# Low parts of 35 weight tiles made by an accumulating DMA in place of a subtraction, in a one-core encoder block

## The chip, the cores and the metric

The kernel runs on one core of a Trainium2 chip. The metric is the device time of one execution in microseconds (us), taken as the median of several runs. The core's engines are TensorE (PE, the matmuls; PEld is its loading of weights), VectorE (DVE), ScalarE (ACT), GpSimd (POOL) and SyncE (SP, which only issues transfers). Each works through its own queue in order; they meet at semaphores. Transfers between device memory and on-chip memory (DMA) run on 16 shared DMA engines and are issued here mostly by SP, a few by GpSimd and ScalarE.

## The reference

One layer of an encoder for 512 tokens of 1024 channels, all in 32-bit floats:

```python
h = _rmsnorm(x, norm_mix[i])
proj = h @ w_in[i]                       # 1024 -> 768 + 256 + 32 + 3 * 512
q = (_rmsnorm(c_q, q_norm[i]) @ w_uq[i])  # latent attention, 8 heads of 96
kv = (_rmsnorm(c_kv, kv_norm[i]) @ w_ukv[i])
y_attn = _block_attention(q, k, v)
y_hyena = x0 * _bidir_long_conv(x1 * vh, h_fwd, h_bwd, hyena_bias[i])
x = x + concat(norm(y_attn), norm(y_hyena)) @ w_out[i]
x = x + (silu(g) * u) @ w_down[i]        # g, u: convolved halves of norm(x) @ w_up
x = x + sigmoid(x @ w_ple_gate[i]) * _rmsnorm(p[i] @ w_ple[i], ple_norm[i])
```

So there are an input projection, attention with a normed latent query and key, a long convolution whose filter comes from a small network (three sine layers), an output projection for both halves, a gated MLP, and an embedding gate.

## The kernel before

**Precision.** TensorE works on `float32r` operands, which hold fewer bits than `float32`. Every matrix operand is therefore cut in two: a high part `hi`, rounded to `float32r`, and a low part `lo = raw - hi`. A product is three matmuls: `hi hi`, `hi lo`, `lo hi` (`prod3`). A tile of weights has 128 partitions and up to 1024 columns; 8 blocks of 128 columns, three matmuls each, are 24 matmuls of 512 tokens.

**The stream of weights.** `stream` lists all weight tiles in the order of use, each with a number of columns `cut`. Tiles 0 to 20 are the input projection (tiles 0 and 1 are loaded in halves by other code at the start), 21 is the keys' projection, 22 to 27 are the queries' (768 columns), 28 is the values', 29 to 36 are the output projection (first the four tiles of the convolution's half, then the four of attention's), 37 to 80 are the MLP's projection up, and then come the projection down, the embedding and the gate. `wload` handles one tile: SP loads it into a raw buffer (L138), ScalarE rounds it into `hi` (L141, named wh in the profile), and the low part (wl) is subtracted, columns up to `cut` on VectorE (L143), the others on GpSimd (L145). For tiles 2 to 36 the list `CUTS` divides the columns between the two engines; from tile 37 on VectorE does all.

**Buffers and lead.** There are three raw buffers and two each for `hi` and `lo`, so the rounding of a tile has to wait until TensorE is done with the tile before the last one. `next_w` hands out a tile and asks for the next one by `ahead(i + 2)`. The filter's output weights (L401) and the transposed embedding take a raw buffer too.

**The order of work.** TensorE's queue is written out by hand: matmuls of the projections, with tasks between them (filter network, transforms, statistics) that come in after a given time of TensorE's, then the attention over eight heads with pieces of the output projection between, then the MLP. The orders on VectorE, ScalarE, GpSimd and SP come from a scheduler that goes by priority; `wload` runs at a priority raised by `WPRI` from the fifth tile on. GpSimd also issues the transfers of the transform's matrices (dft, L499 and L503), `sel` and `selT`, and does products and sums for the convolution, the rotation and the softmax.

**Names that recur.** L175 is the line of all products (`mms`), L131 and L134 are subtractions in `split`, which makes high and low parts of activations, L365 and L375 are a sine layer's matmul and its sine, L412 is the low half of its last output, L403 and L404 sum the filter's output weights, L437 scales the filter in time (the waits of L551 name it), L551 is the transposes for the transform, L596 to L608 are sums after it, L645 and L646 are squares of the latent query, L665 copies the sums of squares that L230 turns, L219 sums squares over channels, L486 to L492 are squares of x.

Of the kernel before, what the change touches and what calls it, by code (L numbers as in the profile page):

```python
# [12 lines left out]
F32 = mybir.dt.float32  # L13
F32R = mybir.dt.float32r
AF = mybir.ActivationFunctionType
ALU = mybir.AluOpType
# [3 lines left out]
P = 128  # L20
# [41 lines left out]
GN = (4, 6, 7, 9)  # L62
CPRI = 50
EPS = 1e-6
NH = 8
# [23 lines left out]
def tile_encoder_block(  # L89
# [6 lines left out]
    V, S, G, PE, SP = nc.vector, nc.scalar, nc.gpsimd, nc.tensor, nc.sync  # L96
# [8 lines left out]
    const = ctx.enter_context(tc.tile_pool(name="const", bufs=1))  # L105
    apool = ctx.enter_context(tc.tile_pool(name="apool", bufs=16))
    wpool = ctx.enter_context(tc.tile_pool(name="wpool", bufs=2))
# [20 lines left out]
    def split(hi, lo, src, g=None):  # L128
        if g is None:
            S.activation(hi, src, AF.Copy)  # L130
            V.tensor_tensor(lo, src, f32(hi), op=ALU.subtract)  # L131
        else:
            S.activation(hi, src, AF.Copy, scale=g)
            V.scalar_tensor_tensor(lo, src, g, f32(hi), op0=ALU.mult, op1=ALU.subtract)  # L134

    def wload(src, n, cut):
        raw = wpool.tile([P, 1024], F32, tag="wr", name="wr", bufs=3)
        SP.dma_start(raw[:, :n], src)  # L138
        hi = wpool.tile([P, 1024], F32R, tag="wh", name="wh")
        lo = wpool.tile([P, 1024], F32R, tag="wl", name="wl")  # L140
        S.activation(hi[:, :n], raw[:, :n], AF.Copy)  # L141
        if cut:
            V.tensor_tensor(lo[:, :cut], raw[:, :cut], f32(hi[:, :cut]), op=ALU.subtract)  # L143
        if cut < n:
            G.tensor_tensor(lo[:, cut:n], raw[:, cut:n], f32(hi[:, cut:n]), op=ALU.subtract)  # L145
        return hi, lo

    stream = [(w_in[m], 1024, CUTS[m]) for m in range(21)]
# [3 lines left out]
    for m in range(8):  # L152
        stream += [(w_down[m][:, o * P : (o + nk) * P], nk * P, nk * P) for o, nk in ((0, 8), (8, 8), (16, 6))]
        if m == 6:
            stream += [(w_ple[0], 1024, 1024), (w_ple[1], 1024, 1024)]
    stream += [(w_gate[m], 1024, 1024) for m in range(8)]
    ready = []
    taken = [0]

    def ahead(i):  # L160
        while len(ready) < min(i, len(stream)):
            with tc.high_priority(offset=WPRI if len(ready) > 3 else 0):
                ready.append(wload(*stream[len(ready)]))

    def next_w():
        i = taken[0]
        taken[0] += 1
        if i:
            ahead(i + 2)
        return ready[i]  # L170
# [29 lines left out]

    # out = v ** -0.5 for v = src / n + EPS
    def rsqrt(out, v, w, src, n, key):
# [19 lines left out]

    # statistics with the tokens on partitions: column 8 t + h for token tile t and head h
    def col(name="col"):
# [21 lines left out]

# [1 line left out]
    p2 = ExitStack()  # L248
# [8 lines left out]
    def single(name, shape=(P, T), dt=F32):  # L257
        return ft.tile(list(shape), dt, tag=name, name=name)

    def first_tile():  # L260
        return [
            wpool.tile([P, 1024], dt, tag=g, name=g, bufs=n)
            for g, dt, n in (("wr", F32, 3), ("wh", F32R, 2), ("wl", F32R, 2))
        ]
# [11 lines left out]
    xraw, halves = [], {}  # L276
    for k in range(8):
        t = xpool.tile([P, T], F32, tag="x", name="x")
# [12 lines left out]
    for k in range(8):  # L291
        h, l = atile(), atile()
# [11 lines left out]
    accx, accy = single("accx"), single("accy")  # L304
# [20 lines left out]
    sel = const.tile([P, 56], F32R, tag="sel", name="sel")  # L325
    selT = const.tile([40, 6, P], F32R, tag="selT", name="selT")

    # work beside the projections: each task continues after the tensor engine's given time
    tasks, clock, serial = [], [0.0], itertools.count()
# [23 lines left out]

    # rotary key part (replicated in the four 32-row groups)
    def rotate(dst, src):
# [5 lines left out]

    # long filter: network, last layer, decay, transform
    def sin_layer(hin, kk, col, bcol):
# [19 lines left out]

    # sums and differences of the even samples' halves, at k = 2p and k = 255 - 2p
    def fold_even(cs, a, b, d0, d1):
# [9 lines left out]
    def filter_task():  # L395
        h = sin_layer(zc[0:33, :], 33, 0, "b1")
        yield D_SIN
        h = sin_layer(h[0:64, :], 64, 1, "b2")
        fw_hl = []
        fwo = wpool.tile([P, 1024], F32, tag="wr", name="wr", bufs=3)  # L400
        SP.dma_start(fwo, fw_out)  # L401
        for op in (ALU.add, ALU.subtract):
            t = tmp()  # L403
# [5 lines left out]
        h = sin_layer(h[0:64, :], 64, 2, "b3")  # L409
# [15 lines left out]
        for i, cs in ((0, "c"), (1, "s")):  # L425
            eo = []
            for jt in range(4):
                ps = filt(i, jt)
                t = tmp()
# [9 lines left out]
                if jt < 2:  # L439
                    h, l = gtile(), gtile()  # L440
# [5 lines left out]
            s, d = tmp(), tmp()  # L446
# [5 lines left out]
            for x, t in ((2, s), (3, d)):  # L452
                h, l = gtile(), gtile()
# [30 lines left out]
    for k in range(8):  # L484
        sq = (accx, accy)[k] if k < 2 else tmp()
        S.activation(sq, xraw[k], AF.Square)  # L486
        if k >= 2:
            if k % 2 == 0:
                last = G.tensor_tensor(accx, accx, sq, op=ALU.add)
# [41 lines left out]

    # hyena projections with their short convolution
    def conv(c, z, w, b, m):
# [12 lines left out]
    def transform_task():  # L546
# [33 lines left out]
        while len(H) < 8:  # L580
            yield 1.0
        # product with the filter's transform
        for j in range(2):
# [14 lines left out]
            yield D_MUL  # L598
        # sums for the inverse's halves
        gce, gco = [U["c", j] for j in range(2)], [U["c2", j] for j in range(2)]  # L600
# [32 lines left out]

    # latent q
    zq = []
# [11 lines left out]

    # queries
    act_table("natural_log_exp_and_others")

    def square(src):
        with pri("sq"):
            sq = single("sq")
            S.activation(sq, src, AF.Square)
            h, l = tmp(F32R), tmp(F32R)
            split(h, l, sq)
        return h, l
# [20 lines left out]

    # keys
    wk = next_w()  # L680
# [95 lines left out]

    # values, token-major, high and low parts beside each other
    wv = next_w()
# [113 lines left out]

# [1 line left out]
    p1 = ExitStack()  # L894
# [144 lines left out]

# [1 line left out]
    fp = ctx.enter_context(tc.tile_pool(name="fp", bufs=1, reuse_waits="tile"))  # L1041
# [28 lines left out]

    # projection down, with the per-layer embedding's projection before its last tile
    ev = []

    def embedding():
        ptr = wpool.tile([P, 1024], F32, tag="wr", name="wr", bufs=3)
        SP.dma_start(ptr, pT)
        ph, pl = (fp.tile([P, 1024], F32R, tag=g, name=g) for g in ("ph", "pl"))
        split(ph, pl, ptr)
        pp = [(ph[:, i * T : (i + 1) * T], pl[:, i * T : (i + 1) * T]) for i in range(2)]
        for m in range(8):  # L1080
            if m % 4 == 0:
                w = next_w()
            ps = ax_ps()
            mms(ps, prod3(wtiles(w, 2, (m % 4) * 256), pp))
            em = tf()
            S.activation(em, ps, AF.Copy)
            if m == 0:
                S.activation(acc7, ps, AF.Square)
            else:
                sq = tt4()  # L1090
                S.activation(sq, ps, AF.Square)  # L1091
                G.tensor_tensor(acc7, acc7, sq, op=ALU.add)  # L1092
            ev.append(em)
# [18 lines left out]
    for m in range(8):  # L1112
# [9 lines left out]
        t = tt4()  # L1122
# [174 lines left out]
```

## Time and profile before

| | |
|---|---|
| Median of three runs | 774.98 us (774.70 to 776.65) |
| Span of the profiled execution, first to last instruction | 774.3 us |
| TensorE busy | 730.1 us (94%) |
| VectorE busy | 531.5 us (69%) |
| ScalarE busy | 356.4 us (46%) |
| GpSimd busy | 250.5 us (32%) |
| DMA, bytes moved | 74.84 MB, 97 GB/s on average |

The page of the profile gives the span of the profiled execution, and no other time of it; the median of the runs lies 0.7 us above that span. A row of a group of instructions reads: line, engine, operation, tiles written and read, shapes, count, busy time and mean of one, and the idle time of the engine just before them with what ended it. A row of the waits reads: engine, tile and line that waited, what it waited for, us in total, times, longest. A row of the stretches has from and to, the length, and for PE, PEld, DVE, ACT and POOL the busy us with the count of instructions; then the granted clock of TensorE as a share of full speed, the busy share of the DMA engines, and GB/s. A row of the order in time has the start, the length, engine, line and tiles, and in brackets the idle time before it. A row of the DMA issues has the count, the size of one and the median us from issue to landing.

### The profile page before, as it was taken

The page shows a single profiled execution, that of the slowest core. Times are in us where ns is not written, and L with a number is a line of the kernel's source. Part 1 is how long each engine was busy: PE and PEld are TensorE (multiplying, and loading weights), DVE is VectorE, ACT ScalarE, POOL GpSimd, SP SyncE. Part 2 cuts the span into 40 slices and gives each one's busy share as a digit, 9 for nine tenths or more (in the row PEclk, how much of TensorE's full clock was granted, in tenths as well). Part 3 has the DMA queues.
Part 4 walks back from the last instruction along what each step waited for, and adds up shares of the span by engine and source line. Part 5 has one row for each costly group of instructions (what it writes and reads, how often), then busy time and mean ns, then how long its engine had stood idle before and what let it go on. Part 6 is the DMA issues. An engine that isn't in the chain of part 4 may idle for free.

```text
span 774.3 us, 8973 instructions
## 1 busy us (share of the span) xinstructions
PE 730.1 (94%) x3254; PEld 584.7 (76%) x3254; DVE 531.5 (69%) x729; ACT 356.4 (46%) x543; POOL 250.5 (32%) x201
## 2 busy tenths in 40 slices
PE   6987989988798989999999999999999999999997
PEld 4765778765467777777888888888888888888886
DVE  6499998899879989786866656666565333233383
ACT  6443343334757977354554443434444122226341
POOL 4356542567355665232232122212222000005000
PEclk9999999989899999999999999999999999999999
DMA  8622332211244210022323232332323333333331
GB/s 280 212 81 83 112 106 83 66 50 41 82 129 115 84 50 28 34 98 89 101 88 109 86 105 87 105 106 85 108 82 103 95 86 108 91 124 102 108 109 55
DMA packets 25504, 74.84 MB, mean 97 GB/s; under 512 B 3402, under 2 KB 3978, under 8 KB 25459
## 3 DMA queue, kind: packets, MB, share of 16 engines
q1 hardware_dynamic: 24418, 71.62, 29.1%
q0 software_dynamic: 784, 2.25, 0.9%
q8 instruction: 25, 0.41, 0.2%
q10 hardware_dynamic: 256, 0.39, 0.2%
q14 instruction: 21, 0.16, 0.1%
HBM read 69.01 MB, written 2.10 MB: 92 GB/s over the span
## 4 chain that ended last, share of the span: by engine, by line
PE 53%; DVE 0%; ACT 0%; DVEq 0%; issue 0%
PE mm L175 36%; PE ax L175 17%; PE ax L219 0%; DVE t L1125 0%; ACT t L1124 0%; DVEq L1292 0%; DVE t L1126 0%
## 5 line engine op out<-in xcount | busy, mean ns | idle before, releaser
L175 PE MATMUL mm<-a,wh 128*128 128x512 f32 (+1 forms) x928 | 291.3, 395 | 8.7 <-ACT wh L272 5.4
L175 PEld LDWEIGHTS mm<-a,wh 128*128 128x128 f32 x928 | 175.1, 191 | 52.4 <-DVE a L134 6.0
L143 DVE TENSOR_TENSOR wl<-wr,wh 128x1024 fp32r<-128x1024 f32 (+3 forms) x106 | 128.9, 1216 | 113.0 <-ACT wh L141 111.0
L141 ACT ACTIVATE wh<-wr 128x1024 fp32r<-128x1024 f32 (+1 forms) x113 | 116.4, 1030 | 152.5 <-PE mm L175 107.4
L175 PE MATMUL mm<-a,wl 128*128 128x512 f32 (+1 forms) x464 | 181.4, 391 | 1.0 <-DVE wl L143 1.0
L175 PE MATMUL ax<-a,wh 128*128 128x512 f32 x384 | 118.2, 389 | 0.0
L175 PEld LDWEIGHTS mm<-a,wl 128*128 128x128 f32 x464 | 88.7, 191 | 20.2 <-DVE wl L143 1.4
L145 POOL TENSOR_TENSOR wl<-wr,wh 128x768 fp32r<-128x768 f32 (+3 forms) x31 | 59.9, 1931 | 85.6 <-ACT wh L141 81.4
L1061 POOL TENSOR_TENSOR f<-f 128x512 f32<-128x512 f32 x22 | 28.7, 1304 | 169.5 <-DVE f L541 149.9
L175 PEld LDWEIGHTS ax<-a,wh 128*128 128x128 f32 x384 | 72.2, 188 | 14.9
L175 PE MATMUL ax<-a,wl 128*128 128x512 f32 x192 | 74.7, 389 | 0.0
L175 PE MATMUL mm<-g,wh 128*128 128x512 f32 x232 | 73.6, 399 | 0.8 <-ACT t L645 0.8
L175 PE MATMUL mm<-h,wh 128*128 128x512 f32 x192 | 59.0, 389 | 0.0
L175 PEld LDWEIGHTS mm<-g,wh 128*128 128x128 f32 x232 | 44.0, 192 | 12.8 <-issue 1.9
L175 PE MATMUL mm<-g,wl 128*128 128x512 f32 x116 | 46.0, 397 | 1.5 <-DVE wl L143 1.5
L1092 POOL TENSOR_TENSOR acc<-acc,t 128x512 f32<-128x512 f32 x7 | 10.0, 1433 | 102.9 <-ACT t L1091 102.4
L175 PEld LDWEIGHTS ax<-a,wl 128*128 128x128 f32 x192 | 36.0, 188 | 7.5
L175 PEld LDWEIGHTS mm<-h,wh 128*128 128x128 f32 x192 | 36.0, 188 | 7.4
L1057 DVE TENSOR_TENSOR f<-mm,R 128x512 f32<-128x512 f32 x22 | 15.2, 691 | 33.9 <-PE mm L175 33.8
L175 PE MATMUL mm<-h,wl 128*128 128x512 f32 x96 | 37.3, 389 | 0.0
L534 ACT ACTIVATE f<-f,par 128x512 f32<-128x512 f32 x44 | 35.4, 807 | 0.7 <-DVE f L1057 0.7
L541 DVE SCALAR_TENSOR_TENSOR f<-f,par 128x511 f32<-128x511 f32 x44 | 33.9, 771 | 1.4
(311 smaller groups left out, 1078.2 us busy)
## 6 DMA issues: line engine op xcount, KB each, us to landing
wr<-in_w_up_dram SPq DMA_DIRECT2D x44, 512.0 KB, 3.5
wr<-in_w_in_dram SPq DMA_DIRECT2D x19, 512.0 KB, 3.3
wr<-in_w_down_dram SPq DMA_DIRECT2D x16, 512.0 KB, 3.5
x<-in_xT_dram SPq DMA_DIRECT2D x16, 256.0 KB, 3.7
wr<-in_w_out_dram SPq DMA_DIRECT2D x8, 512.0 KB, 3.6
wr<-in_w_gate_dram SPq DMA_DIRECT2D x8, 512.0 KB, 3.4
wr<-in_w_down_dram SPq DMA_DIRECT2D x8, 384.0 KB, 3.0
wr<-in_w_uq_dram SPq DMA_DIRECT2D x6, 384.0 KB, 3.0
```

Of the source, the lines that this page charges most:

```text
L141: S.activation(hi[:, :n], raw[:, :n], AF.Copy)
L143: V.tensor_tensor(lo[:, :cut], raw[:, :cut], f32(hi[:, :cut]), op=ALU.subtract)
L145: G.tensor_tensor(lo[:, cut:n], raw[:, cut:n], f32(hi[:, cut:n]), op=ALU.subtract)
L175: last = PE.matmul(out, l, r, start=start and i == 0, stop=stop and i == n - 1)
L534: S.activation(c, z, AF.Identity, scale=pcol(w, 3 * m + 1), bias=pcol(b, m))
L541: V.scalar_tensor_tensor(c[:, 0 : T - 1], z[:, 1:T], pcol(w, 3 * m + 2), c[:, 0 : T - 1], op0=ALU.mult, op1=ALU.add)
L1057: V.tensor_tensor(z, ps_up.pop(m), R2, op=ALU.mult)
L1061: G.tensor_tensor(cc[1], cc[0], cc[1], op=ALU.mult)
L1092: G.tensor_tensor(acc7, acc7, sq, op=ALU.add)
```

## The change

For tiles 2 to 36 the low part is no longer subtracted. ScalarE writes the negated rounded part, `-hi`, into `lo` by a second copy with scale -1, and GpSimd issues a DMA that reads the raw weights once more from device memory and adds them onto `lo`. Tiles from 37 on keep their subtraction on VectorE. The raw tile has then been read for the last time when ScalarE has negated it; raw buffers go from three to two, `hi` and `lo` from two to three each, and a tile is asked for one tile earlier (`ahead(i + 3)`). To make room, `selT` moves to a pool that is given back before the attention, and the squares' own buffer `sq` goes, its place taken by `accy`.

```diff
+NDMA = 37
     def wload(src, n, cut):
-        raw = wpool.tile([P, 1024], F32, tag="wr", name="wr", bufs=3)
+        raw = wpool.tile([P, 1024], F32, tag="wr", name="wr", bufs=2)
         SP.dma_start(raw[:, :n], src)
-        hi = wpool.tile([P, 1024], F32R, tag="wh", name="wh")
-        lo = wpool.tile([P, 1024], F32R, tag="wl", name="wl")
+        hi = wpool.tile([P, 1024], F32R, tag="wh", name="wh", bufs=3)
+        lo = wpool.tile([P, 1024], F32R, tag="wl", name="wl", bufs=3)
         S.activation(hi[:, :n], raw[:, :n], AF.Copy)
+        if cut is None:
+            S.activation(lo[:, :n], raw[:, :n], AF.Copy, scale=-1.0)
+            G.dma_start(lo[:, :n], src, accum_op=ALU.add)
+            return hi, lo
         if cut:
...
+    stream = [(src, n, None if 2 <= i < NDMA else cut) for i, (src, n, cut) in enumerate(stream)]
...
         if i:
-            ahead(i + 2)
+            ahead(i + 3)
...
-    selT = const.tile([40, 6, P], F32R, tag="selT", name="selT")
+    selT = single("selT", (40, 6, P), F32R)
...
         with pri("sq"):
-            sq = single("sq")
-            S.activation(sq, src, AF.Square)
+            S.activation(accy, src, AF.Square)
             h, l = tmp(F32R), tmp(F32R)
-            split(h, l, sq)
+            split(h, l, accy)
```

The other places that allocate a raw, high or low buffer (`first_tile`, the filter's output weights, the embedding) change their counts likewise; some comments go.

More of the change, by code (lines that the diff above doesn't have):

```diff
@@ L262, in first_tile @@
             wpool.tile([P, 1024], dt, tag=g, name=g, bufs=n)
-            for g, dt, n in (("wr", F32, 3), ("wh", F32R, 2), ("wl", F32R, 2))
+            for g, dt, n in (("wr", F32, 2), ("wh", F32R, 3), ("wl", F32R, 3))
         ]
@@ L399, in filter_task @@
         fw_hl = []
-        fwo = wpool.tile([P, 1024], F32, tag="wr", name="wr", bufs=3)
+        fwo = wpool.tile([P, 1024], F32, tag="wr", name="wr", bufs=2)
         SP.dma_start(fwo, fw_out)
@@ L1074, in embedding @@
     def embedding():
-        ptr = wpool.tile([P, 1024], F32, tag="wr", name="wr", bufs=3)
+        ptr = wpool.tile([P, 1024], F32, tag="wr", name="wr", bufs=2)
         SP.dma_start(ptr, pT)
```

## The prediction

> **What bounds the kernel now.** I read the page's first part, then the chain of waits that ended last, then the table of stretches of 20 us, and then what TensorE waited for. The page says that TensorE is busy for 94% of the span and VectorE for 69%:
>
> ```profile
> span 774.3 us, 8973 instructions
> ...
> PE 730.1 (94%) x3254; PEld 584.7 (76%) x3254; DVE 531.5 (69%) x729; ACT 356.4 (46%) x543; POOL 250.5 (32%) x201
> ```
>
> That average hides two regimes. The chain shows the second one:
>
> ```profile
> 358.26 0.04 issue
> ...
> 370.84 5.44 PE ax L175 x24
> ```
>
> From 358.3 us on, the chain is TensorE without a gap, 5.44 us for each weight tile of 24 matmuls, which is 0.227 us a matmul. Nothing that the other engines save can shorten those 416 us. All that the change can win or lose lies ahead of 358 us, and there the table of stretches looks different:
>
> ```profile
> 40.00:60.00 20.00, 17.76 (x66) 13.20 (x66) 19.90 (x27) 7.93 (x10) 11.35 (x11) 0.91 0.22 77
> 60.00:80.00 20.00, 16.04 (x62) 11.87 (x61) 18.79 (x22) 8.46 (x11) 12.73 (x10) 0.91 0.23 80
> ...
> 160.00:180.00 20.00, 16.01 (x58) 12.34 (x57) 18.74 (x20) 6.18 (x10) 11.86 (x7) 0.83 0.19 60
> 180.00:200.00 20.00, 14.97 (x62) 9.27 (x60) 18.82 (x20) 13.00 (x22) 14.09 (x9) 1.00 0.14 39
> ...
> sum 358.00, PE 319.26 PEld 244.33 DVE 308.21 ACT 195.59 POOL 183.07; mean PE 17.74 PEld 13.57 DVE 17.12 ACT 10.87 POOL 10.17
> ```
>
> TensorE idles for 358.0 - 319.3 = 38.7 us in this part. In the stretches shown VectorE (the third pair of numbers) is busy 94 to 99% of the time, ScalarE 31 to 65%. What TensorE waited for between 20 and 358 us:
>
> ```profile
> PE ax L365 <- ACT x L375: 5.6, 2, 4.0
> PE mm L175 <- DVE wl L143: 5.6, 4, 3.2
> PE ax L230 <- ACT t L665: 5.0, 2, 4.3
> PE ax L175 <- DVE ptl L131: 2.3, 3, 1.1
> PE ax L551 <- DVE t L437: 2.1, 1, 2.1
> PE ax L939 <- ACT pr L865: 1.7, 4, 0.8
> PE ax L175 <- DVE g L412: 1.5, 1, 1.5
> ```
>
> Only 5.6 us is waiting for a low part itself (wl). The filter network (L365, L412) and its companions (L551) wait for long VectorE chains, 9.2 us together.
>
> **What is taken away.** The 35 subtractions of weight tiles 2 to 36, in pieces on VectorE (L143) and GpSimd (L145). All stretches from 20 to 345 us, then VectorE from 40 to 120 us alone:
>
> ```profile
> L143 DVE TENSOR_TENSOR wl<-wr,wh 128x256 fp32r<-128x256 f32 (+3 forms) x28 | 29.0, 1037 | 11.1 <-ACT wh L141 10.9
> ```
> ```profile
> L145 POOL TENSOR_TENSOR wl<-wr,wh 128x768 fp32r<-128x768 f32 (+3 forms) x31 | 59.9, 1931 | 85.6 <-ACT wh L141 81.4 <-PE mm L175 4.1
> ```
> ```profile
> L143 DVE TENSOR_TENSOR wl<-wr,wh 128x256 fp32r<-128x256 f32 (+2 forms) x8 | 10.0, 1247 | 1.0 <-ACT wh L141 1.0
> ```
>
> VectorE loses 29.0 us of work, GpSimd 59.9. The waits that name wl on VectorE go: 5.6 us. They lie mostly here (160 to 200 us):
>
> ```profile
> PE mm L175 <- DVE wl L143: 4.7, 3, 3.2
> ```
>
> In these 40 us there are 58 + 62 = 120 matmuls, worth 27.2 us at 0.227, while TensorE is busy for 31.0 and idle for 9.0. The 3.8 us over are slow matmuls after pauses (granted clock 0.83 in the first half). The wl waits are 4.7 of the 9.0 idle us, so I put 4.7/9.0 x 3.8 = 2.0 us of slowness to them. **First term: -5.6 - 2.0 = -7.6 us.**
>
> The chains of the filter network run between 40 and 120 us. There wl takes 10.0 of 80 us of a full VectorE, about as much as the 9.2 us that TensorE waits. Only subtractions that stand inside a chain shorten it, and I can't tell how many do; half of 9.2 is **the second term, -4.6 us.** Its bounds are 0 (none stands there) and -9.2.
>
> Freed work also frees others. The same operation of the same shape on VectorE, undisturbed and while GpSimd worked:
>
> ```profile
> 180.23 0.68 DVE L131 TENSOR_TENSOR t<-sq,t 128x512 fp32r<-128x512 f32 x1
> ...
> 187.44 1.78 DVE L131 TENSOR_TENSOR t<-sq,t 128x512 fp32r<-128x512 f32 x1
> ```
>
> The slow one costs 1.1 us more. If each of the 31 GpSimd subtractions does that once, VectorE gains another 31 x 1.1 = 34 us. I don't add it to the sum, since I can't tell how many of them fall where TensorE waits for VectorE; the rival "more is won" takes it up. The Trainium skill, SBUF — State Buffer, section "Who interferes with whom", states it as a rule: a VectorE instruction with two SBUF inputs and a GpSimd instruction that reads SBUF lock each other out for a whole instruction, and the later one waits. The trace agrees with it by this pair of rows.
>
> Between 240 and 320 us only three weight tiles are made, so the waits on ptl and pr stay: 0.
>
> **What is added on ScalarE.** 35 negated copies, as long as the rounding copies there:
>
> ```profile
> L141 ACT ACTIVATE wh<-wr 128x1024 fp32r<-128x1024 f32 (+1 forms) x35 | 35.7, 1021 | 37.1 <-PE mm L175 35.9 <-issue 1.1
> ```
>
> About 35.7 us more on an engine that was busy for 195.6 of 358. Behind each queue the copies for the short convolution, the sine and the splits. The one long TensorE wait that ScalarE ends is L665 (5.0 us, two times); one more copy ahead of it is **the third term, +1.0 us.** If ScalarE had no room, the cost would be up to 35.7.
>
> **The accumulating DMA and its lead.** No row shows an accumulating DMA. The nearest: plain loads of the same size by SP, and of the same size and type by GpSimd:
>
> ```profile
> wr<-in_w_up_dram SPq DMA_DIRECT2D x44, 512.0 KB, 3.5
> wr<-in_w_in_dram SPq DMA_DIRECT2D x19, 512.0 KB, 3.3
> ...
> dft<-in_c_dft_dram POOLq DMA_DIRECT2D x4, 512.0 KB, 5.1
> ```
> ```profile
> 17.47 1.30 POOL L499 DMA_DIRECT2D dft<-in_c_dft_dram  x2
> 18.75 0.56 POOL L500 DMA_DIRECT2D sel<-in_c_sel_dram  x1
> 19.26 0.56 POOL L501 DMA_DIRECT2D selT<-in_c_selT_dram  x1
> ```
> ```profile
> 12.00:24.00 12.00, 11.96 (x44) 8.55 (x44) 9.95 (x11) 6.59 (x11) 5.93 (x8) 0.86 1.01 319
> ```
>
> The dft loads took 5.1 us while the DMA engines were full (share 1.01, 319 GB/s); their issue costs GpSimd 0.65 us each, a third of the 1.93 us subtraction that goes. From below, an accumulation is a plain load, 3.3 us. From above, everything in it doubles: 2 x 5.1 = 10.2. I take 5.6: 3.3, plus the bytes once more at 319 GB/s (0.524 MB, 1.6 us), since the sum needs what lies in the tile beside the raw weights, plus the 0.65 us of issue. That is nearer to the lower row, because in the stretches quoted above the DMA share is only 0.14 to 0.23.
>
> The Trainium skill, Collectives: The Full Stack, section "The bandwidth ceiling: the fold count and why AG ≠ RS ≠ AR", speaks against the change: a DMA that adds must read two sources, so it delivers bytes at half the rate of a copy. Without that rule the landing would be 3.3 + 0.65 = 4.0 us and the fourth term below 1 instead of 2; no run here shows it yet.
>
> Who covers these 5.6 us? The third buffer for high and low parts, with the raw loads asked one tile further ahead. A slot comes free when TensorE starts tile j-2, and ScalarE then rounds and negates: 2 x 1.05 us, and 5.6 us later tile j may be used. In the tightest packing two tiles are 2 x 5.44 = 10.9 us, and 2.1 + 5.6 = 7.7 fits with 3.2 to spare for queues. Where tiles are shorter (18 matmuls, 768 columns) or late it is tighter. The slot's moment is where today's rounding copy of the tile before stands:
>
> ```profile
> 182.93 0.84 ACT L141 ACTIVATE wh<-wr 128x768 fp32r<-128x768 f32 x1
> ```
> ```profile
> 191.44 0.63 PE L175 MATMUL mm<-g,wh 128*128 128x512 f32 x2
> ```
> ```profile
> 337.50 1.04 ACT L141 ACTIVATE wh<-wr 128x1024 fp32r<-128x1024 f32 x1
> ```
> ```profile
> 346.54 0.62 PE L175 MATMUL mm<-a,wh 128*128 128x512 f32 x2
> ```
>
> That is 8.5 us for tile 24 and 9.0 for tile 36, against 7.3 and 7.7. GpSimd's queue is in order: an issue that comes behind a product of about the length of a subtraction (1.9 us), which itself waits for VectorE, is late by as much, and the products behind an issue that waits for ScalarE are late in turn. **Fourth term: +2.0 us** for one or two such misses.
>
> **The start.** Tile 2 has no lead. Today:
>
> ```profile
> 15.33 1.14 ACT L486 ACTIVATE t<-x 128x512 f32<-128x512 f32 x2
> 20.04 1.06 ACT L141 ACTIVATE wh<-wr 128x1024 fp32r<-128x1024 f32 x1 [3.58 <-PE mm L175]
> ```
> ```profile
> 21.14 1.23 DVE L143 TENSOR_TENSOR wl<-wr,wh 128x1024 fp32r<-128x1024 f32 x1 [0.40 <-ACT wh L141]
> ```
> ```profile
> 23.24 0.39 PE L175 MATMUL mm<-a,wl 128*128 128x512 f32 x1
> ```
>
> The third slot lets rounding start once ScalarE's squares are done, 16.5 us; with the negated copy it is 18.6, and the accumulation lands at 18.6 + 5.6 = 24.2, one microsecond late; if the dft, sel and selT issues (until 19.8) go first, and the 1.05 MB of the two dft loads are ahead in its queue (3.3 us at 319 GB/s), it is 19.8 + 3.3 + 5.6 = 28.7, five late. **Fifth term: +3.0 us**, the middle.
>
> Costed at nothing: two raw buffers for three. In the unbroken part a raw slot is free 2.3 us after its rounding starts (1.05, and 1.23 as tile 2's subtraction above) and refilled in 3.5, while the next use is 10.9 us later. The filter's output weights hold a raw slot from their load until GpSimd has read them:
>
> ```profile
> 31.17 0.33 SPq L401 DMA_DIRECT2D wr<-in_fw_out_dram  x1
> 38.83 24.12 SPq L138 DMA_DIRECT2D wr<-in_w_in_dram  x4
> ```
>
> In that time the other slot alone gives a tile every 3.3 + 2.1 = 5.4 us, and the four raw loads in 24.1 us show that tiles are wanted some 8 us apart; without that cover each tile would cost the difference. selT's and the square's new places change no order.
>
> **Sum:** -7.6 - 4.6 + 1.0 + 2.0 + 3.0 = -6.2. Span 774.3 - 6.2 = 768.1; the runs' median lies 0.7 above the span (774.98), so 768.8, and I say **768.8 us**; its own range is 763 to 773.
>
> **The rivals.** *Late low parts (slower).* The accumulation takes 10.2 us. Then 2.1 + 10.2 + 1.5 for queues = 13.8 us, against 9.0 for tile 36 (4.8 late), 8.5 for tile 24 (its copies are shorter, 13.4: 4.9 late) and 10.9 in a packed run (2.9 late). A late tile gives the next one its lateness as lead, so I count places and not tiles: the start (5), tiles 24 and 36, and three packed runs of 2.9 make 23.4; less the first two terms (12.2), plus 1 on ScalarE, it is 774.98 + 12.2 = 787. It decides from about 8.5 us a DMA upward. For it: no row shows such a DMA. Against: DMA engines are three quarters idle.
> *More is won.* The mutual locks go too, all of 9.2 and the 5.0 us of L665 vanish, the start costs 1: -7.6 - 9.2 - 5.0 + 1 + 1 = -19.8, 755. For it: VectorE at 94 to 99%.
> *The gain is eaten at the start and by GpSimd's order.* The start costs 5, the misses 5, ScalarE 1, against 12.2: 774, no change.
> *It doesn't do what it says:* the issue waits in GpSimd's queue behind products that wait for VectorE, so the wl wait only changes its name. The first term is lost, and start, misses and ScalarE cost 3 + 4 + 1 against 4.6: 779.
>
> **How the numbers follow.** Forecast 0.40, late low parts 0.17, more is won 0.18, eaten 0.13, renamed wait 0.12. Range 754 to 787, from the second rival to the first. The measurement tells 0.3% (2.3 us) from no change. Faster: 0.37 of the forecast, 0.18, and 0.03 of eaten: 0.58. Slower: 0.17 + 0.11 + 0.01 = 0.29. The rest, 0.13, is the same.
>
> **What would show it.** After: no wait of TensorE on wl from VectorE before 358 us, but perhaps on the DMA; DMA issues on GpSimd of 0.65 us and landings near 5 us; VectorE's work 29 us or more below; the filter's waits halved; a gap near 23 us of 1 to 5 us. The unbroken part must start near 352 instead of 358 and last 416 us. Wrong it would be with landings over 8.5 us, with GpSimd issues over 2 us, or if TensorE waits for low parts in the runs of tiles 18 to 24 and 33 to 36.

## The result: one per cent slower

The changed kernel takes **783.64 us** (782.37 to 783.76), the kernel before, beside it on the same chip, 775.82 us. The ratio is 1.0095 with a 95% interval of 1.0072 to 1.0118. The time lies inside the predicted range, but the sign is wrong: 768.8 us was forecast.

From the page of the changed kernel: span, busy times, the DMA queue that GpSimd issues to (packets, MB, share of 16 engines), GpSimd's new group of issues, and the landings of the low parts (median us in the last column).

```profile
span 781.9 us, 8992 instructions
...
PE 733.1 (94%) x3254; PEld 588.6 (75%) x3254; DVE 486.7 (62%) x701; ACT 387.2 (50%) x578; POOL 215.8 (28%) x205
...
q0 software_dynamic: 5824, 19.82, 13.7%
...
L145 POOL DMA_DIRECT2D wl<-in_w_in_dram x19 | 16.6, 874 | 71.7 <-ACT wl L144 71.6
...
wl<-in_w_in_dram POOLq DMA_DIRECT2D x19, 512.0 KB, 8.0
...
wl<-in_w_out_dram POOLq DMA_DIRECT2D x8, 512.0 KB, 7.5
```

The work moved as the change says: VectorE lost 531.5 - 486.7 = 44.8 us, GpSimd 34.7, and ScalarE gained 30.8. The line numbers are those of the new file: L175 is now L181, L665 is L670, L743 to L745 are L748 to L750, L131 and L134 are L132 and L135; L144 is the negated copy and L145 the accumulating DMA. An accumulation lands 8.0 us after its issue, not 5.6 or 5.

The chain of waits shows where the bound changes over:

```profile
366.29 0.73 PE mm L181 x2
367.02 5.46 PE ax L181 x24
```

The unbroken part begins at 366.3 us, 8.0 later than the 358.3 of before. It is 7.6 us of span in all; what follows 366 us is as long as it was. So all of it happened ahead of that, as the prediction expected of any change, and there TensorE now waits for this:

```profile
PE ax L236 <- ACT t L670: 9.6, 2, 5.5
PE mm L181 <- DMA wl<-in_w_in_dram: 5.8, 1, 5.8
PE ax L181 <- DVE t L132: 3.5, 2, 3.1
...
PE mm L181 <- ACT a L134: 2.0, 1, 2.0
PE mm L181 <- DVE a L135: 1.9, 1, 1.9
PE mm L181 <- ACT t L651: 1.6, 1, 1.6
...
PE ax L371 <- ACT x L381: 1.6, 2, 1.4
```

The wait on wl from VectorE is gone. One wait on wl from the DMA is there, at the start, and none later. Of the filter network's waits (9.2 us) L371, 1.6 us, is left. In their place stand L236 with 9.6 us in two waits (its forerunner L230: 5.0; the one of 4.2 us was there before as well, with 4.3) and two waits on `a`, a split that was in time before.

**A ledger of the loss.** The order on TensorE is the same in all kernels told of here, so a matmul of one kernel can be set against the matmul of the same number in another. This table says how many us later than in the kernel before it started (negative: earlier); the columns after the first are experiments described below. One profiled execution scatters: the last column's kernel has the program of the kernel before up to some 230 us, and still stands at -2.2 and -1.0 there.

| matmul no. (us, before) | changed | 2, 3 subtract | output subtracts | buffers only | no addition | 2, 3, 29, 30 subtract | before, other split order |
|---|---|---|---|---|---|---|---|
| 40 (21.0) | -0.6 | -0.2 | -0.1 | 0.3 | -0.5 | -0.4 | 0.0 |
| 60 (25.5) | 7.5 | -0.2 | 7.7 | 0.3 | 5.7 | -0.4 | 0.0 |
| 620 (175.2) | -5.8 | -12.8 | -5.8 | -4.3 | -9.8 | -13.8 | -2.2 |
| 780 (224.1) | -1.5 | -9.0 | -2.2 | -1.0 | -7.5 | -10.0 | -1.0 |
| 820 (234.1) | 7.9 | -2.0 | -1.5 | -0.9 | -1.4 | -9.3 | -1.0 |
| 1000 (269.3) | 7.0 | -2.9 | -1.5 | -1.0 | -2.2 | -10.1 | -1.4 |
| 1040 (277.0) | 12.4 | 2.4 | -1.5 | -1.0 | 4.2 | -4.0 | -1.4 |
| 1340 (337.9) | 9.0 | -0.7 | 3.2 | 5.4 | 0.9 | -7.3 | -1.4 |
| 1500 (376.1) | 8.0 | -1.8 | 2.2 | 4.3 | -0.2 | -8.4 | -1.4 |

The first column reads: 8.0 us lost at the start, 13.3 won by 175 us, 4.4 of them given back by 224 us, **9.4 lost at 224 to 234 us**, 5.4 at 269 to 277 us, and 4.4 won from 277 us on. Of these last 4.4 only some 1.5 are the step at 277 us coming back: the fastest kernel below, which has no such step, wins 2.9 there. Matmul 620 as rows, before and after:

```profile
175.22 0.63 PE L175 MATMUL mm<-ckh,wh 128*128 128x512 f32 x1
```
```profile
169.40 0.39 PE L181 MATMUL mm<-ckh,wh 128*128 128x512 f32 x1
```

In the table of stretches of the changed kernel TensorE (second number) does not idle at all between 100 and 160 us:

```profile
100.00:120.00 20.00, 20.00 (x99) 16.78 (x98) 17.50 (x27) 13.28 (x18) 7.07 (x9) 1.00 0.83 208
120.00:140.00 20.00, 20.00 (x90) 16.57 (x89) 14.62 (x22) 9.22 (x13) 4.26 (x4) 1.00 0.69 155
140.00:160.00 20.00, 20.00 (x90) 16.57 (x89) 16.70 (x25) 9.55 (x12) 9.11 (x7) 1.00 0.57 121
...
220.00:240.00 20.00, 13.30 (x44) 8.04 (x43) 7.85 (x15) 7.86 (x15) 4.00 (x4) 0.77 0.56 132
```

So the change does what it is meant to in the middle, and pays for it at three places.

**Place one, the start.** GpSimd's queue, then ScalarE's, then TensorE's:

```profile
16.90 1.32 POOL L505 DMA_DIRECT2D dft<-in_c_dft_dram  x2
18.18 0.96 POOL L145 DMA_DIRECT2D wl<-in_w_in_dram  x1
```
```profile
16.78 1.04 ACT L144 ACTIVATE wl<-wr 128x1024 fp32r<-128x1024 f32 x1
```
```profile
28.67 0.79 PE L181 MATMUL mm<-a,wl 128*128 128x512 f32 x1 [5.81 <-DMA wl<-in_w_in_dram]
...
30.11 0.63 PE L181 MATMUL mm<-a,wl 128*128 128x512 f32 x1
```

Tile 2 is negated by 17.8 us and its accumulation issued at 18.2, behind two dft loads; it is usable 10.5 us later. TensorE stands for 5.8 us and then runs slowly: from 28.67 to 32.7 us its matmuls take 0.43 us each in place of 0.23, at a granted clock of 0.50, which is the other 2 of the 8.0 us lost. The Trainium skill, TensorE: Matmul & The Clock Gate, section "What's actually happening", states that after an idle window of about 3.4 us the clock halves until a window of that length was busy; the trace agrees with it by these rows (4.0 us at about half speed behind a pause of 5.8).

**Place two, 224 to 234 us.** ScalarE and TensorE in the changed kernel:

```profile
225.20 0.51 ACTq L748 DMA_DIRECT2D kr<-x  x1
...
225.79 0.58 ACTq L749 DMA_DIRECT2D kr<-x  x1
...
233.27 0.63 ACT L750 ACTIVATE ks<-kr 96x512 fp32r<-96x512 f32 x1 [5.58 <-DMA kr<-x]
233.81 0.57 ACT L670 ACTIVATE t<-ax 8x512 f32<-8x512 f32 x1
```
```profile
234.43 0.59 PE L236 MATMUL ax<-ident,t 8*128 8x8 f32 x4 [5.48 <-ACT t L670]
```

And in the kernel before:

```profile
228.90 0.59 ACT L665 ACTIVATE t<-ax 8x512 f32<-8x512 f32 x1 [0.63 <-PE ax L175]
229.39 0.61 ACT L745 ACTIVATE ks<-kr 96x512 fp32r<-96x512 f32 x1
```
```profile
229.54 0.41 PE L230 MATMUL ax<-ident,t 8*128 8x8 f32 x4 [0.68 <-ACT t L665]
```

L670 is a copy of sums of squares that TensorE waits for. Before, it stood ahead of ks, the rounded copy of a head's key; now it stands behind it. ks waits for kr, the head's key put together by two small transfers between on-chip buffers that ScalarE issued itself, and these have become slow. Of the 9.4 us lost, 3.0 come behind the wait, from slow matmuls (the granted clock is 0.77 in the row of 220 to 240 us above). The DMA issues of the changed kernel, and of the one before:

```profile
kr<-x ACTq DMA_DIRECT2D x1, 128.0 KB, 6.8
kr<-x ACTq DMA_DIRECT2D x1, 64.0 KB, 7.4
```
```profile
kr<-x ACTq DMA_DIRECT2D x1, 128.0 KB, 2.2
kr<-x ACTq DMA_DIRECT2D x1, 64.0 KB, 2.0
```

**Place three, 269 to 277 us.** TensorE waits twice for the fourth split of the convolution's half of the output projection:

```profile
282.26 0.50 PE L181 MATMUL mm<-a,wh 128*128 128x512 f32 x1 [1.98 <-ACT a L134]
284.68 0.50 PE L181 MATMUL mm<-a,wh 128*128 128x512 f32 x1 [1.92 <-DVE a L135]
```

On ScalarE this split (L134) now stands behind two rows of the softmax (pr). The first rows are the changed kernel's, the last one is the same split in the kernel before, where it was done long ahead of its use:

```profile
279.46 0.78 ACT L870 ACTIVATE pr<-ax,st,sT 128x512 f32<-128x512 f32 x1
...
280.73 0.78 ACT L870 ACTIVATE pr<-ax,st,sT 128x512 f32<-128x512 f32 x1
...
281.50 0.71 ACT L134 ACTIVATE a<-x,par 128x512 fp32r<-128x512 f32 x1
```
```profile
264.50 0.71 ACT L133 ACTIVATE a<-x,par 128x512 fp32r<-128x512 f32 x1
```

### The profile page after: what moved, and what is told of

Read it like the earlier page. It is cut to its first block, busy times and chain, and to the rows that moved or that the text cites. A ratio compares the mean times of both kernels' runs of the same rounds, so it can differ in the third digit from the quotient of the medians.

```text
span 781.9 us, 8992 instructions
## 1 busy us (share of the span) xinstructions
PE 733.1 (94%) x3254; PEld 588.6 (75%) x3254; DVE 486.7 (62%) x701; ACT 387.2 (50%) x578; POOL 215.8 (28%) x205
## 3 DMA queue, kind: packets, MB, share of 16 engines
q0 software_dynamic: 5824, 19.82, 13.7%
## 4 chain that ended last, share of the span: by engine, by line
PE 53%; DVE 0%; ACT 0%; DVEq 0%; issue 0%
PE mm L181 36%; PE ax L181 17%; PE ax L225 0%; DVE t L1130 0%; ACT t L1129 0%; DVE t L1131 0%; DVEq L1297 0%
## 5 line engine op out<-in xcount | busy, mean ns | idle before, releaser
L181 PE MATMUL mm<-a,wh 128*128 128x512 f32 (+1 forms) x928 | 291.3, 395 | 12.2 <-ACT wh L278 6.0
L181 PEld LDWEIGHTS mm<-a,wh 128*128 128x128 f32 x928 | 175.5, 191 | 55.5 <-DVE a L135 6.7
L181 PE MATMUL mm<-a,wl 128*128 128x512 f32 (+1 forms) x464 | 181.5, 391 | 5.9 <-DMA wl<-in_w_in_dram 5.8
L148 DVE TENSOR_TENSOR wl<-wr,wh 128x1024 fp32r<-128x1024 f32 (+1 forms) x78 | 99.2, 1272 | 101.7 <-ACT wh L142 100.0
L181 PE MATMUL ax<-a,wh 128*128 128x512 f32 x384 | 118.2, 389 | 0.0
L181 PEld LDWEIGHTS mm<-a,wl 128*128 128x128 f32 x464 | 88.6, 191 | 25.2 <-DMA wl<-in_w_in_dram 6.8
L181 PEld LDWEIGHTS ax<-a,wh 128*128 128x128 f32 x384 | 72.1, 188 | 15.0
L181 PE MATMUL mm<-g,wh 128*128 128x512 f32 x232 | 74.9, 405 | 2.3 <-ACT t L651 1.6
L1066 POOL TENSOR_TENSOR f<-f 128x512 f32<-128x512 f32 x22 | 28.7, 1305 | 169.2 <-DVE f L547 149.5
L181 PE MATMUL ax<-a,wl 128*128 128x512 f32 x192 | 74.7, 389 | 0.0
L181 PE MATMUL mm<-h,wh 128*128 128x512 f32 x192 | 59.1, 389 | 0.0
L181 PEld LDWEIGHTS mm<-g,wh 128*128 128x128 f32 x232 | 44.7, 195 | 14.8 <-issue 2.2
L181 PE MATMUL mm<-g,wl 128*128 128x512 f32 x116 | 46.6, 402 | 0.0
L181 PEld LDWEIGHTS mm<-h,wh 128*128 128x128 f32 x192 | 36.0, 188 | 7.5
L181 PEld LDWEIGHTS ax<-a,wl 128*128 128x128 f32 x192 | 36.0, 187 | 7.5
L1097 POOL TENSOR_TENSOR acc<-acc,t 128x512 f32<-128x512 f32 x7 | 10.5, 1498 | 103.5 <-ACT t L1096 103.1
L181 PE MATMUL mm<-h,wl 128*128 128x512 f32 x96 | 37.3, 389 | 0.0
L145 POOL DMA_DIRECT2D wl<-in_w_in_dram x19 | 16.6, 874 | 71.7 <-ACT wl L144 71.6
L1065 ACT ACTIVATE f<-f 128x512 f32<-128x512 f32 x22 | 13.9, 631 | 44.5 <-DVE f L547 44.5
```

Source lines behind the costliest of these rows:

```text
L145: G.dma_start(lo[:, :n], src, accum_op=ALU.add)
L181: last = PE.matmul(out, l, r, start=start and i == 0, stop=stop and i == n - 1)
L1065: S.activation(cc[0], cc[0], AF.Silu)
L1066: G.tensor_tensor(cc[1], cc[0], cc[1], op=ALU.mult)
```

## Experiments

All diffs are against the changed kernel except where another is named. Medians and intervals are against the kernel before on the same chip (776.15 us beside the first four, 776.32 beside the next four, 774.84 beside the last three).

**Tiles 2 and 3 subtract again.**

```diff
-    stream = [(src, n, None if 2 <= i < NDMA else cut) for ...]
+    stream = [(src, n, None if 4 <= i < NDMA else cut) for ...]
```

> Tiles 2 and 3 get their subtractions back, tiles 4 to 36 keep the accumulating DMA. Theory S (the start's loss goes to the end): in the changed kernel the 60th matmul is 8.0 us later, against the kernel before, than the 40th; without tile 2's DMA this step goes, so the unbroken part starts near 358 us instead of 366 and the time is 783.6 - 8 = 775.6. Rival H (later stalls hide it: the filter network's waits take the 8 us up, which shrank by some 6 us where the start was late): the time stays at 781 or above.

Measured: 775.30 us, ratio 1.0002 (0.9984 to 1.0020). In the ledger's second column the start's loss is gone, -0.2 in place of 7.5 at matmul 60, and it stays won. So it is the accumulation of these two tiles, and TensorE's wait names tile 2's. Places two and three are still there (7.0 and 5.3 us).

**The output projection's tiles subtract again.**

```diff
-NDMA = 37
+NDMA = 29
```

> The accumulating DMA ends with tile 28; the eight output tiles keep their subtractions. Theory K (the accumulations of the first two output tiles slow the rotary and key copies between buffers that ScalarE's queue waits for, and the sums of squares stand behind): the copies into kr near 226 us land in 2 to 3 us instead of 7.5, the wait of the transposes on L670 falls from 9.6 to 5 us or less, and with the slow clock behind it the time falls by 9 to about 774.6. Rival O (it is only the order of ScalarE's queue, with the sums behind the key's rounding): the wait stays over 8 us and the time at 782 or above.

Measured: 780.60 us, ratio 1.0063 (1.0039 to 1.0088). The steps at 228 and 277 us are gone (0.7 and 0.0 us) and the wait on L670 is down to 4.0 us, as the theory K expected, but the time is neither theory's: 4.7 us are lost at 277 to 338 us, where the changed kernel wins 3.4. Removing two steps of 9.4 and 5.4 us therefore won only 3.0 us (5.8 in the ledger), and the next experiment says why.

**The buffers and the lead alone, no accumulation.**

```diff
-NDMA = 37
+NDMA = 0
```

> No accumulating DMA at all: only the buffers (two raw, three high and low), the earlier request, selT's and the square's places. Theory W (the 12 to 16 us that TensorE gained between 50 and 175 us came from the work taken off VectorE and GpSimd): this kernel is as the kernel before, 775.8 within 2. Rival L (they came from the third buffer's lead): this kernel is 6 to 16 us faster than before, 760 to 770.

Measured: 780.40 us, ratio 1.0055 (1.0031 to 1.0078), slower than both expectations. At matmul 780 it stands at -1.0, where the kernel with only tiles 2 and 3 subtracting stands at -9.0: the gain in the middle is the accumulating DMA's, some 8 us, and not the third buffer's. Between 277 and 338 us it loses 6.4 us. There TensorE waits for splits of the attention's output:

```profile
PE mm L181 <- DVE a L135: 3.1, 4, 1.3
```

In the kernel before this stretch has one such wait of 0.3 us. With two raw buffers, three of the others and the subtraction kept, these splits come late; with the accumulation (the changed kernel: 12.4 to 9.0 in that stretch) this loss does not occur. VectorE's rows show two differences ahead of these splits: L221, a step of the norm, takes 2.88 us there (0.68 in the kernel before, L215), and a subtraction of 0.68 us stands at 334.69 us between the third split and the last. How much each counts for is not separated.

**A plain DMA in place of the accumulating one.** The low parts are the raw weights then, since nothing is added.

```diff
-            G.dma_start(lo[:, :n], src, accum_op=ALU.add)
+            G.dma_start(lo[:, :n], src)
```

> The same DMA without the addition: it overwrites the low part with the weights themselves (so the low parts are wrong, the addition is left out; every instruction and wait stays). Theory A (the addition is what makes the DMA slow, its packets taking 328 ns of an engine instead of 174): landings fall from 8.0 to about 5 us, DMA share of the first half falls by a third, TensorE's wait on wl from the DMA falls from 5.8 to 3, and the time to 776 to 780. Rival Q (the issue through GpSimd's software queue is what is slow): landings stay over 7 us and the time within 2 us of 783.6.

Measured: 776.16 us, ratio 1.0002 (0.9982 to 1.0022). From its page, and the same queue on the page of the kernel before:

```profile
q0 software_dynamic: 5824, 19.82, 7.5%
...
wl<-in_w_in_dram POOLq DMA_DIRECT2D x19, 512.0 KB, 4.8
...
wl<-in_w_out_dram POOLq DMA_DIRECT2D x8, 512.0 KB, 4.5
```
```profile
q0 software_dynamic: 784, 2.25, 0.9%
```

The same bytes in the same packets land in 4.8 us in place of 8.0. Engine time per packet: without the low parts the queue takes 0.9% x 16 x 774.3 = 111 us. The 5824 - 784 = 5040 packets of low parts take 7.5% x 16 x 773.8 - 111 = 818 us when plain, 162 ns each, and 13.7% x 16 x 781.9 - 111 = 1603 us when adding, **318 ns each: twice as long**. The prediction cited the Trainium skill, Collectives: The Full Stack, section "The bandwidth ceiling: the fold count and why AG ≠ RS ≠ AR": a transfer that adds reads two sources and moves bytes at half the rate. The page says it of the reduce-scatter between cores; this case shows the factor (318 against 162 ns, 1.96) for a queue of GpSimd's, and not its reason. The addition costs 9.3 us by matmul 820 (7.9 against -1.4): 1.9 at the start, 4.2 in the middle, 3.2 at place two. Even a plain DMA loses 6.1 us at the start and 6 at each of the other two places.

**The start's queue.** The dft loads go behind tile 2's accumulation.

```diff
-            G.dma_start(lo[:, :n], src, accum_op=ALU.add)
+            acc.append(G.dma_start(lo[:, :n], src, accum_op=ALU.add))
...
-    with tc.issue_after(last.ins):
+    with tc.issue_after(acc[0].ins):
```

> As the changed kernel, but the eight loads of the transform's table are issued on GpSimd behind tile 2's accumulating DMA, not two of them ahead of it. Theory 'queue at the start' (tile 2 is late because its accumulation stands 1.3 us behind the table's loads and shares the engines with them): the start's loss of 8.0 us falls to 1 to 4 us, and the kernel takes 776 to 780 us, as far as the table's own delay costs nothing. Rival 'the accumulation's own length' (8 us from issue to landing where the subtraction took 1.3): the loss stays at 6 us or more, 782 to 785 us.

Measured: 778.42 us, ratio 1.0038 (1.0017 to 1.0059). GpSimd's queue and TensorE:

```profile
18.14 1.01 POOL L145 DMA_DIRECT2D wl<-in_w_in_dram  x1 [1.14 <-ACT wl L144]
```
```profile
25.45 0.50 PE L182 MATMUL mm<-a,wl 128*128 128x512 f32 x1 [2.56 <-DMA wl<-in_w_in_dram]
```

It was issued at the same time as in the changed kernel (18.14 against 18.18) and yet usable 3.2 us earlier. So not the place of the issue cost it, but the megabyte of dft that was already on its way. From matmul 40 to 60 the loss is 2.9 us in place of 8.0: 5.1 from the dft loads ahead, 2.9 from the accumulation itself. The 5.1 include the 2 us of slow matmuls, for behind this pause of 2.6 us the granted clock stays at 1.0.

**Place two, taken apart: order or bytes.** The first of two kernels changes the order and keeps all bytes. `CPRI` is the scheduler's priority for putting together and rounding the keys and queries of the first two heads (L748 to L751), ks among them:

```diff
-CPRI = 50
+CPRI = 20
```

> All 35 accumulations, bytes and buffers as in the changed kernel; only the planner's constant CPRI is 20 in place of 50, which lets the ScalarE row L670 and its neighbours on VectorE go ahead of ks near 226 us; the orders of TensorE, GpSimd and SyncE are the same. Theory 'order': the step of 9.3 us at 228 us falls below 3 us, and the kernel takes 775 to 778 us. Rival 'contention alone' (the key copies are slow, and what waits for them is late whatever the order): the step stays at 6 us or more and the time at 781 to 785 us. Either way the 8 us of the start stay.

Measured: 779.23 us, ratio 1.0042 (1.0025 to 1.0059). ScalarE:

```profile
228.78 0.59 ACT L670 ACTIVATE t<-ax 8x512 f32<-8x512 f32 x1 [0.28 <-PE ax L181]
...
234.09 0.63 ACT L750 ACTIVATE ks<-kr 96x512 fp32r<-96x512 f32 x1 [3.34 <-DMA kr<-x]
```

The step from matmul 780 to 820 falls from 9.4 to 4.1 us, between the two expectations (below 3, over 6). kr lands as late as in the changed kernel (7.4 to 7.7 us); TensorE now waits for ks itself. The other kernel keeps the order and takes the bytes away from tiles 29 and 30. In the changed kernel GpSimd issued their accumulations just ahead of kr:

```profile
217.25 0.88 POOL L145 DMA_DIRECT2D wl<-in_w_out_dram  x1
...
224.94 0.88 POOL L145 DMA_DIRECT2D wl<-in_w_out_dram  x1 [1.51 <-ACT wl L144]
```

```diff
-            G.dma_start(lo[:, :n], src, accum_op=ALU.add)
+            d = 128 if len(ready) in (29, 30) else n
+            G.dma_start(lo[:, :d], src[:, :d], accum_op=ALU.add)
```

> The order of every engine as in the changed kernel, but the accumulating DMA of tiles 29 and 30 brings 128 of 1024 columns (the addition for the other columns is left out, so these low parts are wrong). Theory 'order and copies' (ks waits for the key copies, and these wait for the DMA engines that the two accumulations hold): the key copies land in 2 to 5 us in place of 7.5, and the step at 228 us falls from 9.3 to 2 to 6 us, so 777 to 781 us. Rival 'order alone': key copies as slow as before, step of 8 us or more, 783 us. Rival 'bytes alone': step below 1 us, 774 to 775 us.

Measured: 779.74 us, ratio 1.0042 (1.0022 to 1.0062). The kernel leaves out the addition for the other 896 columns of these two tiles; its added line shifts the line numbers by one.

```profile
227.70 0.63 ACT L751 ACTIVATE ks<-kr 96x512 fp32r<-96x512 f32 x1 [3.17 <-DMA kr<-x]
228.24 0.57 ACT L671 ACTIVATE t<-ax 8x512 f32<-8x512 f32 x1
```

kr lands in 4.7 to 4.9 us, and the step is 5.5 us. The order is worth 9.4 - 4.1 = 5.3 us, the bytes 9.4 - 5.5 = 3.9, together 9.2 of 9.4. Neither "contention alone" nor "order alone" holds. Most of what is left of kr's delay is not the accumulations': in the kernel with the buffers alone, where nothing accumulates, the smaller transfer into kr took 4.5 us as well. With the new buffers a raw load of 512 KB went out 0.1 us from it, in the kernel before 0.4 us behind it, when it took 2.0; whether that is the reason was not tested.

```profile
kr<-x ACTq DMA_DIRECT2D x1, 64.0 KB, 4.5
```

**Both gone: tiles 29 and 30 subtract too.**

```diff
-    stream = [(src, n, None if 2 <= i < NDMA else cut) for ...]
+    stream = [(src, n, None if 4 <= i < NDMA and i not in (29, 30) else cut) for ...]
```

> Low parts of tiles 2, 3, 29 and 30 are made by subtraction as in the kernel before, all other 31 of the 35 by the accumulating DMA; the buffers are those of the change. This puts the ScalarE row of the mixer's norm (L670) back ahead of the scaling ks, which waits for the key copies. Theory 'order and copies' (the changed kernel loses 8.0 us at its start and 9.3 us at 228 us; the latter comes from L670 standing behind ks, the former from tile 2): the gain of the middle (9.0 us by record 780, as in the run without tiles 2 and 3) is kept past 234 us and no step of more than 2 us appears there; about 767 us (763 to 770), ratio 0.985 to 0.993. Rival 'the output tiles cost it whichever way' (the buffers alone lost 5.7 us at 328 to 338 us): the gain is given back at the attention's end, about 772 to 776 us. Rival 'accumulations of the tiles near by': the step at 228 us stays at 6 us or more, 775 us.

Measured: **768.01 us**, ratio 0.9900 (0.9875 to 0.9925). Without the two negated copies L670 is back ahead of ks, the step at 228 us is 0.7 us, and the loss at 277 to 338 us that the subtracting output tiles had doesn't come. Place three stays, 6.1 us, with the same two waits on the split.

**Place three: the order of the split.** `'so'` is the scheduler's priority for the splits of the convolution's half. Against the kernel just told of:

```diff
-PRI = {... 'so': -300, ...}
+PRI = {... 'so': -200, ...}
```

> The run without tiles 2, 3, 29 and 30 (768.0 us) with one constant of the planner besides: the priority of the split of yh ('so') is -200 in place of -300, which puts the fourth split on ScalarE and VectorE back ahead of the two softmax rows behind which it stands in that run; the order of TensorE is the same. Theory 'order of the split' (TensorE's step of 6.2 us between 269 and 277 us is the wait for that split): the step falls below 1 us; some 2 us of it were given back by 304 us anyway, so about 764 us (762 to 766). Rival 'the output weights come late' (the step is the accumulating DMA of the output tiles): step and time stay, 768 us.

Measured: **762.82 us** (762.64 to 763.91), ratio 0.9842 (0.9821 to 0.9862), the fastest of all. The page and the chain:

```profile
span 761.0 us, 8994 instructions
```
```profile
345.34 0.73 PE mm L181 x2
```

Matmul 1040 stands at -10.0 like matmul 1000: the step was the wait for that split, whose place the scheduler had moved. On ScalarE the fourth split starts at 254.49 us in place of 264.34. The span falls from 765.6 to 761.0, so a step of 6.1 us had cost 4.6 at the end. The unbroken part starts at 345.3 us, 13.0 earlier than before. The output tiles' accumulations are the same in both kernels, so they were not what was late.

**The same constant in the kernel before.**

```diff
-PRI = {... 'so': -300, ...}
+PRI = {... 'so': -200, ...}
```

> The kernel before, with the same constant -200 in place of -300 and nothing else. It has no step at 277 us, since its fourth split stands in time; if the gain of the mended kernel comes from the low parts and not from the constant, this takes 774 to 778 us, no change. Rival 'the constant is a gain of its own': 772 us or less, and the mended kernel has to be compared with this one.

Measured: 775.08 us, ratio 0.9999 (0.9984 to 1.0013). The constant wins nothing by itself; the 12 us are won by the rest of the change. As its buffers and lead alone lost 4 us, that is the way the low parts are made.

**All bytes from tile 4 on, with both orders put right.**

```diff
-PRI = {... 'so': -300, ...}
+PRI = {... 'so': -200, ...}
-CPRI = 50
+CPRI = 20
...
-    stream = [(src, n, None if 2 <= i < NDMA else cut) for ...]
+    stream = [(src, n, None if 4 <= i < NDMA else cut) for ...]
```

> Tiles 2 and 3 subtract, all 33 others have the accumulating DMA, tiles 29 and 30 among them; the priority of the split is -200 and CPRI is 20, so both orders of ScalarE (L670 ahead of ks, the fourth split ahead of the softmax rows) are as in the kernel before although every byte of the change from tile 4 on is moved. Theory 'order': the steps at 228 and 277 us stay below 3 us together, 764 to 768 us. Rival 'bytes' (the two accumulations slow the key copies, and that decides): a step of 5 us or more at 228 us, 770 us or more.

Measured: 767.34 us, ratio 0.9904 (0.9878 to 0.9929). Against 762.82 it loses 4.5 us, and its step from matmul 780 to 820 is 4.1 us (-8.7 to -4.6), as in the run with `CPRI` 20 alone. That is between the two expectations: the time fits "order", the step is that of the bytes. Taking tiles 29 and 30 out is what removes both.

## Why the prediction was wrong, step by step

The step that failed is the third term: the copies added on ScalarE were priced by their length, +1.0 us, and cost 9.4 us at one place and 5.4 at another by the order that they changed and by the transfers beside them. The fifth term, the start, was mis-sized besides: +3.0, measured 8.0.

- **Where the time is decided: right.** Nothing changed after the unbroken part's start; all of the 7.6 us lie ahead of it.
- **First and second term, -12.2: right in kind, the size in part by chance.** Between matmul 60 and 620 the changed kernel wins 13.3 us, the best kernel 13.5. But the kernel with the buffers alone wins 4.6 there, and a kernel with the program of before 2.3, so what the work taken away is worth lies nearer to 9 to 11. The wait on wl from VectorE is gone, and the filter's waits of 9.2 us shrink to 1.6 (L371). The split of the sum between the two terms was not tested. VectorE's work fell by 44.8 us, of which the subtractions' own group is 29.7 (128.9 to 99.2); the other 15.1 are shorter instructions, the effect that the rival "more is won" counted with up to 34. The Trainium skill's rule on locks between VectorE and GpSimd (SBUF — State Buffer, "Who interferes with whom") would do this; no run here separates it.
- **Landing, 5.6 us: wrong, 8.0.** The price of the bytes once more was put at 1.6 us, by the rate of the fullest stretch; the addition cost 8.0 - 4.8 = 3.2, and the plain landing was 4.8 and not 4.0. The issue was not dearer than put: its row is 0.87 us long, but the next issue on GpSimd starts 0.56 us after it (18.18 and 18.74 us).
- **Fourth term, +2.0 for late tiles: did not occur.** Even with 8.0 us no tile after tile 2 was late for TensorE; the lead of 10.9 us covers it. "Late low parts" put its threshold at 8.5 us, and the landing stayed just short of it. That its 787 us is near the measured time is chance: of its places only the start was real. From 175 to 224 us, though, 4.4 us are given back, and the waits on L651 (1.6 us) and L132 (3.1 at once) stand there; the kernel with the buffers alone waits for L651 too (6.0 us) and gives back 3.4 us in that stretch, so most of it is not the accumulations'. Their cause is open. The middle in all is 7.5 + 1.5 = 9.0 us of gain, against 12.2 - 1 - 2 = 9.2 in the sum; that the two agree is chance, since neither the 1 nor the 2 is what was lost there.
- **Fifth term, the start, +3.0: mis-sized, 8.0.** Its upper case, a landing behind the dft loads at 28.7 us, is what happened; that it agrees to the tenth (28.67) is luck, for the issue went out at 18.2 us and not 19.8, and then took 10.5 us and not 8.9. The middle of two cases was taken where the queue can only be in one of them, and the 2 us of slow matmuls behind the pause, which the first term counted at another place, were left out here.
- **Third term, +1.0 for ScalarE: the step that failed.** It was set at the right wait (L665, now L670), as one more copy ahead of it. But the copies changed ScalarE's order, not just its length: L670 fell behind ks, which waits for a transfer. That is 5.3 us, and the accumulations' bytes, which the sum charged to no other transfer, make this one 6.8 to 7.4 us long in place of 4.7 to 4.9, another 3.9. Of the orders only GpSimd's was thought of as a price, not ScalarE's or VectorE's; the same mechanism at the fourth split cost 5.4 us more, of which some 1.5 came back.
- **"Costed at nothing": the buffers.** By themselves they cost 4 us (780.40), at the output tiles, though not in the changed kernel, where these tiles don't subtract.
- **Two small slips.** The rival "it doesn't do what it says" adds up to 778.4 and not 779. And the 0.7 us between span and time set the median beside the span of another execution: in every execution on record the time lies 1.7 to 2.3 us above its own span, so a span of 768.1 would be about 770.

Sum of the ledger, rounded: start +8.0, middle -9.0, place two +9.4, 234 to 269 us -0.9, place three +5.4, from 277 us on -4.4, less the 0.5 that matmul 40 was early: 8.0.

## What to carry to other kernels

An operation moved to another engine was paid for here in that engine's order, more than in its busy time: when a scheduler lays out the queues, set the new order beside the old one around each wait of the bounding engine before believing any sum. Work handed to the DMA engines should be kept out of stretches where they are full (a start) or where a short transfer stands in a chain (the key's copies); here four of 35 tiles taken out, with one priority put right, turned a loss of 1% into a gain of 1.6%.

## What the hardware showed that was not expected

- An accumulating DMA holds an engine for 318 ns a packet against 162 ns for the plain one, and lands 512 KB in 8.0 us against 4.8.
- A 64 KB transfer between on-chip buffers took 7.4 us beside an accumulation and a raw load (DMA engines 56% busy on average, 220 to 240 us), 4.9 when the accumulation brought an eighth of the bytes, 4.5 beside a raw load with no accumulation at all, and 2.0 in the kernel before. So the accumulation's own part is some 3 us.
